# Large experts after small ones: holding back splits until the small expert's last turn, and building one-hot columns a chunk earlier

## Chip, cores, metric

The kernel runs on one core of a Trainium2 chip. The metric is the device time of one execution in microseconds (us).

## What is computed

Two layers of a decoder trunk over 256 tokens of width 1024. Each layer has a mixer (retention, a state-space layer and latent attention side by side) and a feed-forward part. The change lies in the feed-forward part of the second layer, which routes each token to 2 of 8 experts:

```python
def swiglu(h, wg, wu, wd):
    return (jax.nn.silu(h @ wg) * (h @ wu)) @ wd

# routed_ffn, cut
logits = (t @ router)                       # t: 256 x 1024, router: 1024 x 8
top_v, top_i = lax.top_k(logits, 2)
top_w = jax.nn.softmax(top_v, axis=-1)
# the rows of t are gathered by expert; every expert e computes
#   swiglu(rows, wg[e], wu[e], wd[e])       # 1024 -> 3584 -> 1024
# and y[token] += result * weight
```

Each expert has three weight matrices of 1024 x 3584 or 3584 x 1024 in f32, 44 MB for one expert and 352 MB for all eight. All are read once.

## The kernel before

**Slots.** Expert 0 and the seven others, ordered by how many tokens they got, fill eight slots, called experts 0 to 7 here. `KINDS` says which are small (64 columns of tokens: 0, 5, 6, 7) and which large (128 columns: 1 to 4). They are worked off in the order `TURNS`, 0, 1, 2, 5, 3, 6, 4, 7. Three times a large expert follows a small one: 1 after 0, 3 after 5, 4 after 6.

**Chunks.** An expert is done in 7 chunks of 512 of its 3584 inner columns. A chunk reads six pieces of 1 MB: two of `mg` (gate), two of `mu` (up), two of `md` (down). The loop over `turns` in `moe` is a software pipeline written out by hand. One turn does: the gate product of the chunk (`up('mg', ...)`) and Silu of it into `sg` on ACT; the transposes of the previous chunk's hidden rows, `raw_turn` for a small expert (copy `hts` on ACT) or `turn` for a large one (`th` on ACT, `tl` on DVE); the up product (`up('mu', ...)`) and `h = sg * up` on DVE; then the down product of the previous chunk (`raw_down` or `half_down`). After an expert's last chunk `y_parts` (`yh` on ACT, `yl` on DVE) and `scatter` add its result to `acc`. Every engine runs its instructions in the order in which the program issues them.

**Large experts work with split weights.** A small expert multiplies with the f32 pieces as they are. For a large one each half of a piece is first split into two parts, `wh` (cast on ACT) and `wl` (difference on DVE), in `split_half`; each product is then three matmuls (lines 733 to 735). Splits run ahead of their use: `ahead` issues them in the fixed order `porder` as long as fewer than `NH` = 5 halves are alive and the load of the piece has been issued. It is called whenever a half is used up (`w_half`, `w_done`), and with 4 at a small expert's last chunk. In the first chunk of a large expert after a small one, the four halves of `mg` and four of `mu` are split by this, and then, at the end of the gate product, one half of the gate piece of chunk 1. In the ACT queue that cast stands ahead of Silu and of the small expert's last `hts`.

**Loads.** `Stream.pump` issues the loads of pieces on the SP queue in the order of their use. There are 5 staging buffers and 2 more in this stage. One comes free when both halves of its piece are split, or when a small expert's matmuls have read it.

**One-hot columns.** `onehots` builds a 0/1 matrix `gm` on DVE from the slots' positions (one instruction for each of two halves of the tokens). `big_x` and `small_x` gather an expert's tokens with it, as generators of which `advance` runs a step at a time from the list `work`. `side(r)` builds it once more for expert r at chunk 5 (chunk 6 for expert 0) and lets PE transpose it (line 1571) and multiply it with the weights (1572, 1573); the result, `gt` and `ws`, serves `scatter`. The first entry of a turn's `work` runs right after Silu is issued, ahead of the transposes; the others after `h`.

Of the kernel before, what the change touches and what calls it, by code (L numbers as in the profile page):

```python
# [226 lines left out]
class Kernel:  # L227
# [49 lines left out]
    def ahead(self, n=1, E=None):  # L277

        if self.stream.dry:
            return  # L280
        while n and self.pnext < 2 * len(self.porder):
            if self.plive >= self.NH or not self.stream.loaded(self.porder[self.pnext // 2]):
                return
            self.emit_split(E)
            n -= 1

    def emit_split(self, E=None):
        i, j = divmod(self.pnext, 2)
        key = self.porder[i]
        self.parts.setdefault(key, []).append(self.split_half(self.stream.tiles[key][0][0], j, E))  # L290
        self.plive += 1
        self.pnext += 1
        if j:
            self.stream.done(key)
# [18 lines left out]
    def w_done(self, key, ahead=9):  # L313
        if self.stream.dry:
            return
        self.plive -= len(self.parts.pop(key))
        if ahead:
            self.ahead(ahead)

    def w_half(self, key, ahead=9):  # L320

        if self.stream.dry:
            return
        self.parts[key].pop(0)
        self.plive -= 1
        if ahead:
            self.ahead(ahead)
# [1326 lines left out]
    def moe(self, l):  # L1654
        V, S, T = self.V, self.S, self.T
        A, B = self.mod[l, 'Af'], self.mod[l, 'Bf']
        route = self.route(A, B)
        next(route)
        NC = self.NC
        small = lambda r: self.KINDS[r] == 's'  # L1660
        order = self.TURNS
        xg, gts, ys, over = {}, {}, {}, []

        def big_x(r, n):

            X = [self.wkt([128, 8, 256], name, F32R) for name in ("xgh", "xgl")]
            for j in range(n):
                xg[r + j] = [x[:, :, j * 128:(j + 1) * 128] for x in X]
            return self.gather(self.onehots(self.pm[:, :, r:r + n], n, 128), n * 128, A, B, X)

        def small_x(r, n):
            if r:
                x = self.wk.tile([128, 8, n * 64], F32, name="xs")
            else:

                x = self.acc.rearrange("p t d -> p (t d)")[:, :512].rearrange("p (k n) -> p k n", k=8)
            for j in range(n):
                xg[r + j] = x[:, :, j * 64:(j + 1) * 64]
            return self.gather(self.onehots(self.pm[:, :, r:r + n], n, 64), n * 64, A, B, [x])

        def side(r):
            n, w = (2, 64) if small(r) else (1, 128)
            g = self.onehots(self.pm[:, :, r:r + 1].to_broadcast([128, 2, n]), n, w)
            gts[r] = self.slot_side(g, 0, self.wt[:, 0, r:r + 1], self.wt[:, 1, r:r + 1])

        def up(name, r, c, ahead=9):
            p = self.bank("a")
            for i in range(2):
                if small(r):
                    key, w = self.raw_piece(name, c, i, r)  # L1690
                    self.raw_up(p, xg[r], w, i)
                    self.stream.done(key)
                else:
                    key, wh, wl = self.ffn_piece(name, c, i, r)
                    self.half_up(p, xg[r], wh, wl, i, lambda: self.w_half(key))
                    self.w_done(key)
            return p

        self.drain(small_x(0, 1))
        gens = {}  # L1700

        def advance(name, make):
            def f():
                if name not in gens:
                    gens[name] = make()
                next(gens[name], None)
            return f


        work = {(0, 0): [lambda: self.drain(route)],  # L1710
                (0, 1): [lambda: over.extend(self.overflow_list()), self.know_places],
                (0, 2): [advance('s', lambda: small_x(5, 3))] * 3, (0, 3): [advance('s', lambda: small_x(5, 3))] * 3}
        for r in order:
            work.setdefault((r, 5 if r != order[0] else 6), []).append(lambda r=r: side(r))
        for at, b in ((0, 1), (5, 3)):
            for c in (4, 5) if at == 0 else (2, 3):
                work.setdefault((at, c), []).extend([advance(b, lambda b=b: big_x(b, 2))] * 3)

        turns = [(r, c) for r in order for c in range(NC)]
        prev, pend, last = None, [], len(turns) - 1  # L1720
        banks = {}
        free = 'b' + 'dbbb' + 'b' + 'db' + 'b' + 'db' + 'b'
        i = 0
        for r in order:
            n = 1 if small(r) else 2
            banks[r], i = free[i:i + n], i + n

        def scattered(r):
            gt, ws = gts[r]
            if small(r):  # L1730
                yp = self.y_parts(ys[r][0], ws)
                for h in range(2):
                    pend.extend(self.scatter(yp, gt, h, r == 0, slice(64 * h, 64 * h + 64)))

        for n in range(len(turns) + 1):
            cur = turns[n] if n <= last else None
            todo = list(work.get(cur, ()))
            if cur:
                r, c = cur
                w = 256 if small(r) else 512  # L1740
                pg = up('mg', r, c)
                sg = self.wkt([128, 512], "sg")[:, :w]
                S.activation(sg, pg[:, :w], AF.Silu)  # L1743
            if pend:
                pend.pop(0)()
            elif todo:
                todo.pop(0)()
            if prev is not None:
                pr, pc, ph = prev
                ht = (self.raw_turn if small(pr) else self.turn)(ph)  # L1750
            if cur:
                pu = up('mu', r, c)
                h = self.wkt([128, 512], "h")[:, :w]
                V.tensor_mul(h, sg, pu[:, :w])  # L1754
                if small(r) and c == NC - 1 and n < last:
                    self.ahead(4)
            for _ in range(2):
                if pend:
                    pend.pop(0)()
            for f in todo:  # L1760
                f()
            if prev is not None:
                if pc == 0:
                    ys[pr] = [self.bank(t) for t in banks[pr]]
                if small(pr):
                    ps = [self.raw_piece('md', pc, i, pr) for i in range(2)]
                    self.raw_down(ys[pr][0], ht, [w for _, w in ps], pc == 0, pc == NC - 1)
                    for key, _ in ps:
                        self.stream.done(key)
                else:  # L1770
                    for i in range(2):
                        key, wh, wl = self.ffn_piece('md', pc, i, pr)
                        self.half_down(ys[pr][i], ht, wh, wl, pc == 0, pc == NC - 1, lambda: self.w_half(key))
                        self.w_done(key)
                        if pc == NC - 1:
                            gt, ws = gts[pr]
                            pend.extend(self.scatter(self.y_parts(ys[pr][i], ws), gt, i))
                if pc == NC - 1:
                    scattered(pr)
                    for d in (xg, gts, ys):  # L1780
                        d.pop(pr)
            if cur:
                prev = (r, c, h)
        while pend:
            pend.pop(0)()
        self.overflow(A, B, *over)
        o = self.a['out'].rearrange("o (t p) d -> p (o t) d", p=128)
        room = [self.wkt([128, 2, D], name) for name in ("psq", "pyg")]
        for t in range(2):
            hs = [slice(h * 512, (h + 1) * 512) for h in range(2)]  # L1790
            post = self.post(t, [self.acc[:, t, h] for h in hs], self.mod[l, 'Gf'], [r[:, t] for r in room])
            for h, _ in zip(hs, post):
                self.nc.sync.dma_start(o[:, t, h], self.x[:, t, h])
        self.dump(f'xf{l}', self.x.rearrange("p t n -> p (t n)"))
# [89 lines left out]
    def run(self, upto=9):  # L1884
        tc = self.tc
        with ExitStack() as ctx:
# [5 lines left out]
            self.psum = pool(name="psum", bufs=4, space=bass.MemoryType.PSUM)  # L1892
            ctx.enter_context(tc.manual_schedule())
            self.P, self.mod, self.s5, self.b4 = {}, {}, {}, {}
            self.tail = None
            self.c_all, self.c_s5 = ctx, ctx.enter_context(ExitStack())
            self.s5p = self.c_s5.enter_context(tc.tile_pool(name="s5p", bufs=1, side="right"))
# [82 lines left out]
```

## Time and profile before

| | us |
|---|---|
| median of 3 runs | 1485.74 |
| lowest, highest | 1483.95, 1491.18 |
| profiled execution | 1491.5 |
| its span | 1489.7 |

The expert stage begins near 603 us of the span and ends near 1478. The profile shows one execution; times in it count from the start of its span. PE is the matrix engine, ACT casts and does Silu, DVE does elementwise work, SP issues the loads. "PEclk" is the granted clock of PE as a share of 2.4 GHz; 0.50 is 1.2 GHz. In a row of the time order the bracket at the end gives how long the engine was idle before it and what ended that.

### The profile page before, as it was taken

How to read it: one execution, taken by the hardware profiler on the slowest of the kernel's cores; microseconds unless marked ns; L12 is line 12 of the kernel's file. 1: busy time of each engine (PE TensorE's matmuls, PEld its weight loads, DVE VectorE, ACT ScalarE, POOL GpSimd, SP SyncE). 2: the span in 40 equal slices, each digit the busy share in tenths (PEclk: the TensorE clock that was granted, in tenths of full speed). 3: DMA queues.
4: the chain of work that ended last, by engine and by line, in shares of the span. 5: the costliest groups of instructions: out<-in, count | busy, mean ns of one | idle time of the engine just before them, and what ended most of it. 6: DMA issues, size and time to landing. Idle time of an engine off the chain costs nothing. (4 is left out here: it accounts for less than half of the span.)

```text
span 1489.7 us, 21982 instructions
## 1 busy us (share of the span) xinstructions
PE 1390.6 (93%) x8563; PEld 1042.6 (70%) x8563; DVE 848.3 (57%) x1201; ACT 675.4 (45%) x936; POOL 108.9 (7%) x108
## 2 busy tenths in 40 slices
PE   4799789999998999999999999999999998999995
PEld 1676579999997867665687887755687655687652
DVE  4763556656565546313898898522797403897302
ACT  1423444444445244113787877412676202786101
POOL 3201010515021001000000000000000000000000
PEclk9899999999999999799999999999999999999998
DMA  9667794545556484699999998999999999999995
GB/s 305 245 232 277 270 311 183 183 170 172 190 196 242 183 348 184 243 424 424 425 424 403 346 375 334 365 415 425 424 425 378 365 424 425 424 425 354 376 425 207
DMA packets 70078, 482.23 MB, mean 324 GB/s; under 512 B 9800, under 2 KB 10056, under 8 KB 13008
## 3 DMA queue, kind: packets, MB, share of 16 engines
q1 hardware_dynamic: 65952, 473.69, 80.2%
q0 software_dynamic: 3024, 4.75, 1.2%
q10 hardware_dynamic: 992, 2.33, 0.5%
q8 instruction: 69, 1.13, 0.3%
q14 instruction: 41, 0.34, 0.1%
HBM read 479.66 MB, written 1.06 MB: 323 GB/s over the span
## 5 line engine op out<-in xcount | busy, mean ns | idle before, releaser
L274 DVE TENSOR_TENSOR wl<-st,wh 128x1024 fp32r<-128x1024 f32 x464 | 569.6, 1248 | 192.9 <-ACT wh L273 170.0
L273 ACT CAST wh<-st 128x1024 fp32r<-128x1024 f32 x464 | 482.9, 1052 | 274.8 <-PE a L1306 86.4
L733 PE MATMUL a<-wh,xgh 128*128 128x512 f32 x448 | 180.5, 403 | 0.0
L734 PE MATMUL a<-wl,xgh 128*128 128x512 f32 x448 | 177.3, 396 | 2.7 <-DVE wl L274 2.7
L735 PE MATMUL a<-wh,xgl 128*128 128x512 f32 x448 | 176.7, 394 | 0.0
L1593 PE MATMUL a<-st,xs 128*64 128x256 f32 x1344 | 155.1, 381 | 0.9 <-DMA st<-in_mu 0.9
L1593 PEld LDWEIGHTS a<-st,xs 128*64 128x64 f32 x1344 | 95.4, 137 | 57.4 <-issue 12.4
L1305 PE MATMUL a<-hh,wh 128*128 128x256 f32 x448 | 128.2, 286 | 1.9 <-ACT hh L710 1.2
L1743 ACT ACTIVATE sg<-a 128x256 f32<-128x256 f32 (+1 forms) x56 | 27.3, 488 | 224.1 <-PE a L1593 224.1
L1754 DVE TENSOR_TENSOR h<-sg,a 128x256 f32<-128x256 f32 (+1 forms) x56 | 30.8, 551 | 172.1 <-PE a L1593 130.1
L1306 PE MATMUL a<-hl,wh 128*128 128x256 f32 x448 | 127.6, 285 | 0.4 <-DVE hl L711 0.4
L1307 PE MATMUL a<-hh,wl 128*128 128x256 f32 x448 | 127.4, 284 | 0.0
L1610 PE MATMUL b<-st,hts 128*64 128x512 f32 x448 | 110.7, 618 | 13.8 <-ACT hts L1602 9.9
L733 PEld LDWEIGHTS a<-wh,xgh 128*128 128x128 f32 x448 | 85.6, 191 | 22.2 <-issue 2.8
L734 PEld LDWEIGHTS a<-wl,xgh 128*128 128x128 f32 x448 | 85.7, 191 | 21.0 <-DVE wl L274 4.1
L735 PEld LDWEIGHTS a<-wh,xgl 128*128 128x128 f32 x448 | 85.6, 191 | 18.5
L1305 PEld LDWEIGHTS a<-hh,wh 128*128 128x128 f32 x448 | 86.6, 193 | 2.9 <-ACT hh L710 1.4
L1306 PEld LDWEIGHTS a<-hl,wh 128*128 128x128 f32 x448 | 86.6, 193 | 0.8 <-DVE hl L711 0.6
L1307 PEld LDWEIGHTS a<-hh,wl 128*128 128x128 f32 x448 | 86.7, 194 | 0.0
L1610 PEld LDWEIGHTS b<-st,hts 128*64 128x64 f32 x448 | 34.4, 141 | 73.2 <-issue 52.2
L474 PE MATMUL d<-st,c 128*32 128x512 f32 x384 | 53.4, 656 | 23.3 <-DMA st<-in_ada_w 12.1
L337 POOL TENSOR_TENSOR pss<-pss,mhalf 128x1 f32<-128x1 f32 x8 | 5.2, 649 | 890.1 <-DVE pss L336 890.1
(424 smaller groups left out, 1993.7 us busy)
## 6 DMA issues: line engine op xcount, KB each, us to landing
st<-in_mg SPq DMA_DIRECT2D x112, 1024.0 KB, 12.9
st<-in_mu SPq DMA_DIRECT2D x112, 1024.0 KB, 11.6
st<-in_md SPq DMA_DIRECT2D x112, 1024.0 KB, 12.7
st<-in_ada_w SPq DMA_DIRECT2D x48, 1024.0 KB, 7.8
st<-in_fg SPq DMA_DIRECT2D x14, 1024.0 KB, 4.8
st<-in_fu SPq DMA_DIRECT2D x14, 1024.0 KB, 4.8
st<-in_fd SPq DMA_DIRECT2D x14, 1024.0 KB, 4.7
st<-in_w_out SPq DMA_DIRECT2D x8, 1024.0 KB, 7.2
```

The costliest lines, as they stand in the source:

```text
L273: self.S.copy(hi, src)
L274: (E or self.V).tensor_sub(lo, src, hi.bitcast(F32))
L474: self.T.matmul(state['p'][32 * g:32 * g + 32, :], self.c32[:, k, :], st[:, 0, g * 512:(g + 1) * 512], start=(k == 0), stop=(k == 7), skip ...
L733: self.T.matmul(out, xh, wh, start=start, stop=False, skip_group_check=True)
L734: self.T.matmul(out, xh, wl, start=False, stop=False, skip_group_check=True)
L735: self.T.matmul(out, xl, wh, start=False, stop=stop, skip_group_check=True)
L1305: T.matmul(o, wh[:, k, fs], hh[:, kk], start=st, stop=False, skip_group_check=True)
L1306: T.matmul(o, wh[:, k, fs], hl[:, kk], start=False, stop=False, skip_group_check=True)
L1307: T.matmul(o, wl[:, k, fs], hh[:, kk], start=False, stop=(kk == 7), skip_group_check=True)
L1593: self.T.matmul(p[64 * t:64 * t + 64, :256], x[:, 4 * i + k], w[:, k, 256 * t:256 * t + 256], start=(i == 0 and k == 0), stop=(i == 1 and ...
L1610: self.T.matmul(y[64 * i:64 * i + 64, :], ht[:, f % 2, s], ws[i][:, f], start=(first and f == 0), stop=(last and f == 3), skip_group_check ...
L1754: V.tensor_mul(h, sg, pu[:, :w])
```

## The change

Two things are changed in `moe`.

First, when a turn works on a large expert and the previous turn on a small one, `split_up_to` sets a cap, `self.cap`, before the gate product: `ahead` issues no split past the second `mu` piece of that chunk. Once the transposes of the small expert's last chunk and `hts` are issued, the cap is lifted. Splits that a product asks for itself (`w_piece`) don't look at it.

Second, the building of `gm` is parted from its use. `side_hot(r)` does `onehots` in the chunk before the one in which `side(r)` uses it. `big_x` and `small_x` yield between `onehots` and the first step of the gather.

```diff
-        while n and self.pnext < 2 * len(self.porder):
+        while n and self.pnext < min(2 * len(self.porder), self.cap):
...
+    def split_up_to(self, key=None):
+
+        self.cap = 1 << 30 if key is None or self.stream.dry else 2 * self.porder.index(key) + 2
...
-            return self.gather(self.onehots(self.pm[:, :, r:r + n], n, 128), n * 128, A, B, X)
+            g = self.onehots(self.pm[:, :, r:r + n], n, 128)
+            yield
+            yield from self.gather(g, n * 128, A, B, X)
...
-            return self.gather(self.onehots(self.pm[:, :, r:r + n], n, 64), n * 64, A, B, [x])
+            g = self.onehots(self.pm[:, :, r:r + n], n, 64)
+            yield
+            yield from self.gather(g, n * 64, A, B, [x])
+
+        def side_hot(r):
+            n, w = (2, 64) if small(r) else (1, 128)
+            gts[r] = self.onehots(self.pm[:, :, r:r + 1].to_broadcast([128, 2, n]), n, w)
 
         def side(r):
-            n, w = (2, 64) if small(r) else (1, 128)
-            g = self.onehots(self.pm[:, :, r:r + 1].to_broadcast([128, 2, n]), n, w)
-            gts[r] = self.slot_side(g, 0, self.wt[:, 0, r:r + 1], self.wt[:, 1, r:r + 1])
+            gts[r] = self.slot_side(gts[r], 0, self.wt[:, 0, r:r + 1], self.wt[:, 1, r:r + 1])
...
         for r in order:
-            work.setdefault((r, 5 if r != order[0] else 6), []).append(lambda r=r: side(r))
+            c = 5 if r != order[0] else 6
+            work.setdefault((r, c - 1), []).append(lambda r=r: side_hot(r))
+            work.setdefault((r, c), []).append(lambda r=r: side(r))
...
                 w = 256 if small(r) else 512
+                if prev is not None and small(prev[0]) and not small(r):
+                    self.split_up_to(self.ffn_args('mu', c, 1, r)[0])
                 pg = up('mg', r, c)
...
                 ht = (self.raw_turn if small(pr) else self.turn)(ph)
+                self.split_up_to()
```

## Rows read from the trace of the kernel before

**Rows 1.** The page, busy time: engine, busy us and share, instructions.
```profile
PE 1390.6 (93%) x8563; PEld 1042.6 (70%) x8563; DVE 848.3 (57%) x1201; ACT 675.4 (45%) x936; POOL 108.9 (7%) x108
```

**Rows 2.** Stretches of the expert stage: length, engines' busy us, clock, DMA share, GB/s.
```profile
804.00:968.00 164.00, 160.87 (x784) 128.45 (x783) 132.23 (x127) 113.17 (x122) 0.00 (x0) 0.99 0.92 357
...
1136.00:1168.00 32.00, 32.00 (x155) 25.34 (x154) 24.69 (x22) 21.01 (x22) 0.00 (x0) 0.96 0.81 305
1168.00:1354.00 186.00, 177.16 (x982) 120.06 (x981) 95.80 (x98) 81.56 (x98) 0.00 (x0) 0.97 1.01 424
1354.00:1390.00 36.00, 36.00 (x188) 28.02 (x188) 25.53 (x24) 21.87 (x23) 0.00 (x0) 0.96 0.80 304
1390.00:1466.00 76.00, 73.61 (x528) 41.62 (x524) 7.51 (x15) 6.25 (x16) 0.00 (x0) 1.00 1.01 424
```

**Rows 3.** Waits of PE, 600 to 1490 us: us in total, times, longest.
```profile
PE a L1571 <- DVE gm L1522: 10.4, 4, 2.6
PE b L1610 <- ACT hts L1602: 9.9, 4, 3.2
```

**Rows 4.** ACT in order of time, Silu of chunks: start us, duration us.
```profile
790.14 0.59 ACT L1743 ACTIVATE sg<-a 128x512 f32<-128x512 f32 x1
...
810.48 0.59 ACT L1743 ACTIVATE sg<-a 128x512 f32<-128x512 f32 x1
...
913.99 0.59 ACT L1743 ACTIVATE sg<-a 128x512 f32<-128x512 f32 x1
...
935.93 0.59 ACT L1743 ACTIVATE sg<-a 128x512 f32<-128x512 f32 x1
...
1130.55 0.59 ACT L1743 ACTIVATE sg<-a 128x512 f32<-128x512 f32 x1
...
1153.87 0.58 ACT L1743 ACTIVATE sg<-a 128x512 f32<-128x512 f32 x1
...
1332.12 0.59 ACT L1743 ACTIVATE sg<-a 128x512 f32<-128x512 f32 x1
...
1348.90 0.59 ACT L1743 ACTIVATE sg<-a 128x512 f32<-128x512 f32 x1
...
1372.29 0.58 ACT L1743 ACTIVATE sg<-a 128x512 f32<-128x512 f32 x1
```

**Rows 5.** PE in order of time, chunk 5 of expert 1.
```profile
791.75 0.53 PE L1571 MATMUL a<-kc,gm 128*128 128x128 f32 x2 [2.60 <-DVE gm L1522]
...
792.48 0.64 PE L1617 MATMUL a<-kc,h 128*128 128x128 f32 x4
```

**Rows 6.** Stretches around the fourth such wait, columns as in rows 2.
```profile
1332.10:1348.90 16.80, 15.81 (x70) 12.75 (x68) 15.73 (x15) 13.54 (x16) 0.00 (x0) 1.00 1.01 425
...
1352.00:1356.00 4.00, 4.00 (x12) 3.23 (x11) 0.69 (x1) 1.51 (x4) 0.00 (x0) 0.50 0.94 391
```

**Rows 7.** ACT in order of time, from expert 6 to 4.
```profile
1264.13 1.05 ACT L273 CAST wh<-st 128x1024 fp32r<-128x1024 f32 x1 [5.36 <-DMA st<-in_mg]
...
1265.58 0.37 ACT L1602 COPY hts<-a 128x256 f32<-128x256 f32 x1
...
1269.10 1.05 ACT L273 CAST wh<-st 128x1024 fp32r<-128x1024 f32 x1 [0.32 <-DMA st<-in_mu]
```

**Rows 8.** PE in order of time, last down product of experts 0, 5 and 6.
```profile
710.10 3.65 PE L1610 MATMUL b<-st,hts 128*64 128x512 f32 x16 [3.18 <-ACT hts L1602]
...
1048.86 5.35 PE L1610 MATMUL b<-st,hts 128*64 128x512 f32 x16 [3.09 <-ACT hts L1602]
...
1265.99 6.55 PE L1610 MATMUL b<-st,hts 128*64 128x512 f32 x16 [3.11 <-ACT hts L1602]
...
1278.14 0.49 PE L1645 MATMUL a<-yh,gt 64*128 64x512 f32 x1
```

**Rows 9.** DVE in order of time, from expert 6 to 4.
```profile
1266.92 4.63 DVE L274 TENSOR_TENSOR wl<-st,wh 128x1024 fp32r<-128x1024 f32 x4 [0.48 <-ACT wh L273]
1271.47 0.68 DVE L1754 TENSOR_TENSOR h<-sg,a 128x512 f32<-128x512 f32 x1
1273.35 0.75 DVE L1636 SCALAR_TENSOR_TENSOR yl<-b,ws,yh 128x512 fp32r<-128x512 f32 x1 [1.20 <-ACT yh L1635]
```

More of the change, by code (lines that the diff above doesn't have):

```diff
@@ L1894, in run @@
             self.P, self.mod, self.s5, self.b4 = {}, {}, {}, {}
+            self.cap = 1 << 30
             self.tail = None
```

## Prediction, made before the changed kernel was run

> **What bounds the kernel now.** I read the busy shares first: PE is busy 93% of the span [rows 1], which seems to leave little to win. That figure is an average over stages with different limits, so I next read the expert stage in stretches [rows 2]. Look at the last three columns: the granted clock, the share of the DMA engines and the rate. From 1168 to 1354 us and from 1390 to 1466 us the queue of weights runs flat out, at 424 GB/s; the last piece lands near 1468 us and the kernel ends 21 us later. So the end is set by the stream of weights. The stream has a fixed number of bytes, and only the time in which it was not running can be saved. There are three such stretches, all where large experts are at work: 804 to 968 us at 357 GB/s, 1136 to 1168 us at 305, 1354 to 1390 us at 304. Against 424.5 that is (1 - 357/424.5) x 164 = 26.1 us, 9.0 us and 10.2 us of lost transfer. In these stretches PE is busy almost without a break: a staging buffer is free only once its piece has been split, a split needs a buffer that PE gives back, so the stream waits for PE. A stall of PE in a large expert, within such a stretch or before it, delays the stream by its length, up to the transfer that was lost there; elsewhere it costs nothing.
>
> Then I asked which stalls PE has in these experts. The waits of PE name two that belong to the change: 10.4 us in 4 waits for the one-hot columns (gm), and 9.9 us, nearly all of it in three waits, for the ACT copy hts [rows 3].
>
> **Part one: one-hot columns a chunk ahead.** The starts of Silu give the pitch of the chunks [rows 4]. An ordinary chunk of a large expert takes 1348.90 - 1332.12 = 16.78 us. The chunk in which `side` runs takes 810.48 - 790.14 = 20.34 us for expert 1, 21.94 for expert 2, 23.32 for expert 3, 23.39 for expert 4. What `side` adds to PE by itself, from its first transpose to the transposes of `turn`, is 792.48 - 791.75 = 0.73 us, and before it PE sat idle for 2.60 us until DVE had built gm behind its queue of splits [rows 5]. For expert 1 these two explain the longer chunk: 16.78 + 2.60 + 0.73 = 20.1. For experts 2 to 4 there is more: after the stall the granted clock is 0.50, which is 1.2 GHz instead of 2.4, while before it PE ran on at full clock [rows 6]. Built one chunk earlier, the two DVE instructions (0.5 us) lie in the same queue behind the same kind of splits, a whole chunk of 16.78 us before they are read. The stall goes, and with it what sets the clock back. Each such chunk should take 16.78 + 0.73 = 17.5 us, so the gains are 2.8, 4.4, 5.8 and 5.9 us. What the move costs: 0.5 us of DVE in the chunk before, behind which `tl` waits; `tl` is needed only after the 5.6 us of the next mu product, so I cost it at nothing, and at 0.5 us per expert if that cover were gone. For the small experts and for the gathers (`big_x`, `small_x`) the same move lies in stretches where the stream is flat out, so it is worth nothing either way. The gathers used five of their six calls, so the extra yield fits.
>
> **Part two: no fifth split before the small expert's last turn.** At a change from a small to a large expert the ACT queue holds a split of mg for chunk 1 ahead of Silu and ahead of hts. Its weights come late: in expert 4 it starts at 1264.13 us, when the piece has landed, and hts at 1265.58 [rows 7]. PE ended the mu product of chunk 0 at 1265.99 - 3.11 = 1262.88 and stood until hts was there [rows 8]. What would be late next? The `md` pieces of the small expert lie just ahead of that mg piece. Landings are (1269.10 - 1264.13)/2 = 2.5 us apart, so the later `md` piece landed near 1261.6, before PE needs it. Hence `raw_down` could start at 1262.9. It takes 3.65 us at full clock (expert 1), but 5.35 and 6.55 us after the stalls of experts 3 and 4, where the clock fell [rows 8]. So it would end at 1266.5 instead of 1272.5. The next product, mg of chunk 1, runs 1278.14 - 1272.54 = 5.6 us [rows 8]. Its first half would be cast from 1264.13 on, and as Silu and hts no longer stand between the casts, DVE's splits (4 in 4.63 us, [rows 9]) come a little before PE wants them; PE would reach the scatter at 1272.1. There a new, short wait appears: DVE has to split the first half of mu (landed 1269.10, cast 1.05, about 1.2 on DVE: 1271.4), then `h` 0.68 and `yl` 0.75 [rows 9], so the scatter's second matmul may start at about 1272.8, some 0.5 us late. The gains: expert 1, 3.18 - 0.6 = 2.5 us; expert 3, 3.09 + (5.35 - 3.65) - 0.6 = 4.2 us; expert 4, 3.11 + (6.55 - 3.65) - 0.5 = 5.5 us. What the cap takes away is one split run ahead; as the piece lands 5.4 us after ACT ran out of work, that split can't start earlier anyway. The upper end is without the new wait, 0.6 us more each; the lower end, with the wait for mg's splits taking the old one's place, is about 1 us each.
>
> **The sum.** Up to the end of the first lossy stretch (experts 1 and 2): 2.5 + 2.8 + 4.4 = 9.7 us, less than its 26.1, so all of it counts. Expert 3: 4.2 + 5.8 = 10.0 us, but only 9.0 us of transfer were lost: 9.0. Expert 4: 5.5 + 5.9 = 11.4, of which 10.2 count. Together 28.9 us. The profiled execution took 1491.5 us (span 1489.7 and 1.8 around it); 28.9 less is 1462.6. The median of the runs is 1485.7, which gives 1456.8. The two differ by 5.8 us, perhaps because the clock falls in fewer places in some executions; those falls are part of what I subtract, so I subtract from the middle, 1488.6, here and for the rivals: **1460 us**.
>
> The Trainium skill (Perfetto Trace Analysis, Roofline) puts the ceiling of one core's 16 DMA engines at about 435 GB/s. By that figure the two later stretches would have lost 9.6 and 10.8 us instead of 9.0 and 10.2, and the sum would be 30.1. The flat-out rows show 424, which I keep.
>
> **The rivals.**
> *A new wait in place of hts* (1 us gained at each change of expert): 8.2 + 6.8 + 6.9 = 21.9 us, about 1467 us. For it: mg of chunk 1 starts as soon as its first half is split, and the split chain of ACT and DVE begins at the landing, which doesn't move. Against it: at the same pace PE's needs come later than each split.
> *The clock falls anyway*: then only the idle time itself is won, 2.6 us per `side` and 2.5 per change of expert: 7.7 + 5.1 + 5.1 = 17.9 us, about 1471 us. For it: PE still waits for landings at the start of each large expert, a few us before. Against it: through those waits the rows show no fall before the hts stall.
> *One part does not do what it says*: the one-hot part alone gives 18.9, about 1470 us; the cap alone 12.2, about 1476 us.
> *No change*: the lost transfer is not PE's doing but the issuing queue's, and the stream ends when it did. For it: the rate in the lossy stretches is spread over many small dips. Against it: the same queue holds 424 elsewhere.
> *Slower*: with less waiting in large experts, PE meets the small ones with a shorter lead and waits more for landings between their products; the clock falls there. I estimate a small chunk on PE at three products like `raw_down`'s 3.65 us [rows 8], 11 us at full clock, against 14.8 us of the stream (6 landings of 2.5); at half clock some 21, so each chunk caught loses about 6 us. From five such chunks on the gain is gone; eight give 1460 + 48, about 1508 us. Against it: from 1390 to 1466 us, where PE runs small chunks beside a flat-out stream, the clock stays 1.00 [rows 2].
> The Trainium skill (TensorE: Matmul & The Clock Gate, "HAM oscillation") describes such a case, a DMA wait between bursts that sends each next burst to half rate; by that rule this rival would hold, and the last row just named doesn't agree.
>
> **How the numbers follow.** Forecast 0.62, a new wait 0.12, the clock 0.10, one part only 0.06, no change 0.06, slower 0.04. The forecast's own range is 1452 (the median's base, no new waits and no cap by the lost transfer: 1485.7 - 10.3 - 10.6 - 12.0 = 1452.8) to 1466; to hold 8 in 10 I reach to the clock rival: 1452 to 1472. A difference under 0.5% (7.4 us) is about what a measurement of this kernel can't tell from none. Faster by more: 0.62 + 0.12 + 0.10 + 0.06 = 0.90; within it 0.06; slower 0.04.
>
> **What would show it.** In the changed profile: no PE wait for gm in the four large experts and Silu pitches of 17.5 us there; hts on ACT before the first cast of mg's chunk 1, and `raw_down` of about 3.65 us in all three places; clock 1.00 in both; the stream at 424 GB/s nearly throughout from 968 us on, with under 3 us lost. I am wrong if the pitch of those chunks falls but the last landing doesn't move by as much, or if PE stands before mg of chunk 1 instead.

## The result and the profile after

The changed kernel took 1463.54 us (median of 5 executions, 1456.0 to 1465.86) against 1485.74 before: a ratio of 0.9831, 95% interval 0.9804 to 0.9858. In a second comparison, with 19 executions of before, it took 1462.76 against 1491.73: 0.9806, interval 0.977 to 0.9842. (The ratios here and below are those on record; they are not always the quotient of the two medians, which is 0.985 for the first.) It is 22 us faster by the first median, 29 us by the second; the difference lies in the executions of before, which go from 1484 to 1491 us in the first and from 1481 to 1501 us in the second. The profiled execution took 1456.0 us, its span is 1454.2.

The page, busy time, after, against [rows 1]:

```profile
PE 1371.3 (94%) x8563; PEld 1028.3 (71%) x8563; DVE 844.2 (58%) x1201; ACT 672.8 (46%) x936; POOL 108.8 (7%) x108
```

PE does the same matmuls in 19.3 us less. 12.6 us of that lie between the first and the last Silu of the stage, where no step of 4 us shows a clock under 0.99 any more; the other 6.7 us lie ahead of the first Silu. Stretches of the expert stage after, with the columns of [rows 2]:

```profile
804.00:968.00 164.00, 162.41 (x837) 126.51 (x837) 125.68 (x126) 104.88 (x116) 0.00 (x0) 1.00 0.97 384
968.00:1136.00 168.00, 167.88 (x899) 121.26 (x896) 114.98 (x115) 100.40 (x118) 0.00 (x0) 1.00 1.01 424
1136.00:1168.00 32.00, 32.00 (x226) 19.71 (x227) 7.56 (x11) 4.47 (x9) 0.00 (x0) 1.00 1.01 424
1168.00:1354.00 186.00, 181.47 (x988) 128.38 (x985) 114.62 (x113) 98.79 (x113) 0.00 (x0) 1.00 1.01 424
1354.00:1390.00 36.00, 36.00 (x260) 21.29 (x260) 5.00 (x8) 3.65 (x8) 0.00 (x0) 1.00 1.01 425
```

The last column shows where the gain came from. The two later stretches that lost transfer, 305 and 304 GB/s in [rows 2], are gone: from 968 us on the stream of weights runs at 424. Around experts 1 and 2 it rose from 357 to 384 and still loses. Counted in steps of 4 us from 20 us after the first Silu to 8 us after the last, each with (1 - rate/424.5) x 4 and never less than nothing, the stage lost 49.2 us of transfer before and 19.5 after: 29.7 us. The clock column is 1.00 in all five rows.

Waits of PE after, 600 to 1460 us; nothing as long as the two waits of [rows 3] is left:

```profile
PE b L1614 <- DMA st<-in_md: 3.9, 4, 1.3
...
PE a L1545 <- DVE gm L1526: 1.0, 1, 1.0
...
PE b L1614 <- ACT hts L1606: 0.5, 1, 0.5
```

The wait for gm at `side` (10.4 us) is gone altogether; the 1.0 us belongs to a gather. Silu starts of expert 4 after, against the last three of [rows 4]:

```profile
1300.75 0.59 ACT L1757 ACTIVATE sg<-a 128x512 f32<-128x512 f32 x1
...
1317.54 0.59 ACT L1757 ACTIVATE sg<-a 128x512 f32<-128x512 f32 x1
...
1334.94 0.59 ACT L1757 ACTIVATE sg<-a 128x512 f32<-128x512 f32 x1
```

16.79 us for an ordinary chunk, 17.40 for the one with `side`, which was 23.39. From expert 6 to expert 4 after, first ACT, then PE, then DVE, against [rows 7], [rows 8] and [rows 9]:

```profile
1233.45 0.36 ACT L1606 COPY hts<-a 128x256 f32<-128x256 f32 x1
1238.38 1.99 ACT L273 CAST wh<-st 128x1024 fp32r<-128x1024 f32 x2 [4.58 <-DMA st<-in_mg]
```

```profile
1237.06 3.65 PE L1614 MATMUL b<-st,hts 128*64 128x512 f32 x16
...
1246.31 0.50 PE L1649 MATMUL a<-yh,gt 64*128 64x512 f32 x1
1247.02 0.50 PE L1649 MATMUL a<-yl,gt 64*128 64x512 f32 x1 [0.21 <-DVE yl L1640]
```

```profile
1245.62 0.68 DVE L1769 TENSOR_TENSOR h<-sg,a 128x512 f32<-128x512 f32 x1
1246.22 0.74 DVE L1640 SCALAR_TENSOR_TENSOR yl<-b,ws,yh 128x512 fp32r<-128x512 f32 x1
```

hts stands 5 us ahead of the cast that had been before it; `raw_down` starts when the mu product ends and takes 3.65 us instead of 6.55. The short new wait for `yl` is there, 0.21 us here.

### The profile page after: what moved, and what is told of

Read it like the earlier page. It is cut to its first block, busy times and chain, and to the rows that moved or that the text cites. A ratio compares the mean times of both kernels' runs of the same rounds, so it can differ in the third digit from the quotient of the medians.

```text
span 1454.2 us, 21979 instructions
## 1 busy us (share of the span) xinstructions
PE 1371.3 (94%) x8563; PEld 1028.3 (71%) x8563; DVE 844.2 (58%) x1201; ACT 672.8 (46%) x936; POOL 108.8 (7%) x108
## 3 DMA queue, kind: packets, MB, share of 16 engines
HBM read 479.66 MB, written 1.06 MB: 331 GB/s over the span
## 5 line engine op out<-in xcount | busy, mean ns | idle before, releaser
L1614 PE MATMUL b<-st,hts 128*64 128x512 f32 x448 | 106.2, 596 | 6.4 <-DMA st<-in_md 3.9
L739 PEld LDWEIGHTS a<-wh,xgl 128*128 128x128 f32 x448 | 84.1, 188 | 17.9
## 6 DMA issues: line engine op xcount, KB each, us to landing
st<-in_mu SPq DMA_DIRECT2D x112, 1024.0 KB, 14.8
```

What stands on the lines that cost most here:

```text
L739: self.T.matmul(out, xl, wh, start=False, stop=stop, skip_group_check=True)
L1614: self.T.matmul(y[64 * i:64 * i + 64, :], ht[:, f % 2, s], ws[i][:, f], start=(first and f == 0), stop=(last and f == 3), skip_group_check ...
```

## The experiments

All were compared with the kernel before; the first four ran together, and so did the last four, without the changed kernel; what they are said to be over it is counted from its 1462.76 us. "Lost transfer" is counted in steps of 4 us as above. "Stage" is the time from the first Silu (expert 0, chunk 0) to expert 7's first Silu, read from the trace.

**The changed kernel again.**

> The changed kernel as it is, to have more executions and a second trace. My account: in the expert stage, from the first Silu to the Silu of expert 7's first chunk, 31 to 33 us less than in the trace of before (770.7 us there), in this execution as in the first; the chunks with side at 17.4 us; what differs between executions of this kernel (1456 to 1466 us) lies ahead of the first Silu, which came at 611.0 us in the first trace and 615.6 in that of before. Rival: the executions differ inside the expert stage, because the clock falls in some of them at other places; then the stage is 5 to 9 us longer here and a chunk or two shows a granted clock of 0.5. The median over before should stay at 1463 against 1486, 22 to 23 us less.

Median 1462.76 us. First Silu of expert 0 and of expert 7, from the trace of before:

```profile
615.61 0.38 ACT L1743 ACTIVATE sg<-a 128x256 f32<-128x256 f32 x1 [4.47 <-PE a L1593]
...
1386.31 0.39 ACT L1743 ACTIVATE sg<-a 128x256 f32<-128x256 f32 x1 [3.92 <-PE a L1593]
```

from the first trace of the changed kernel:

```profile
611.01 0.38 ACT L1757 ACTIVATE sg<-a 128x256 f32<-128x256 f32 x1 [4.55 <-PE a L1597]
...
1348.97 0.38 ACT L1757 ACTIVATE sg<-a 128x256 f32<-128x256 f32 x1 [3.92 <-PE a L1597]
```

and from the second:

```profile
614.08 0.38 ACT L1757 ACTIVATE sg<-a 128x256 f32<-128x256 f32 x1 [4.72 <-PE a L1597]
...
1353.59 0.38 ACT L1757 ACTIVATE sg<-a 128x256 f32<-128x256 f32 x1 [3.92 <-PE a L1597]
```

The stage takes 738.0 and 739.5 us, against 770.7 before: 31 to 33 us less, as expected. The spans differ by 6.0 us: 3.1 ahead of the first Silu, 1.5 in the stage, the rest behind it. So about half of the difference between these two lies ahead of the stage that was changed. The clock falls nowhere in the stage. One wait is longer than in the first trace, that for `yl` at the change to expert 4:

```profile
1251.63 0.50 PE L1649 MATMUL a<-yl,gt 64*128 64x512 f32 x1 [1.06 <-DVE yl L1640]
```

In the ten traces of this study the first Silu comes between 611.0 and 620.6 us.

**Only the one-hot columns.**

```diff
-                if prev is not None and small(prev[0]) and not small(r):
-                    self.split_up_to(self.ffn_args('mu', c, 1, r)[0])
```

> The changed kernel without the cap: only the one-hot columns are built a chunk ahead. My account: the four chunks with side fall to 17.4 us, 2.9 + 4.5 + 5.9 + 6.0 = 19.4 us less than before by their pitches, and all of it reaches the end, as each stretch that lost transfer lost more than that: 17 to 20 us faster than before. The three waits for hts stay at 3.1 us each, with the clock falling after those at experts 3 and 4. Rival (the stream takes it back, or the falls come anyway): under 12 us.

1475.62 us, 16.1 less than before (ratio 0.988, interval 0.9834 to 0.9926). The four chunks with `side` have 17.4 us; 31.1 us of transfer are lost, 18.1 less than before. The three waits for hts, PE in order of time:

```profile
712.34 6.55 PE L1614 MATMUL b<-st,hts 128*64 128x512 f32 x16 [3.18 <-ACT hts L1606]
...
1046.49 5.03 PE L1614 MATMUL b<-st,hts 128*64 128x512 f32 x16 [3.09 <-ACT hts L1606]
...
1257.28 5.35 PE L1614 MATMUL b<-st,hts 128*64 128x512 f32 x16 [3.12 <-ACT hts L1606]
```

They stay, and this time the clock fell after all three, after the first as well (0.50 from 712 to 716 us), which it had not done in the trace of before. The median gain of 16.1 us is a little under the expected 17 to 20; the recorded ratio makes it 17.9, and in the trace the stage is 18.3 us shorter than before. The rival (under 12 us) is out by the trace; the interval alone, 11 to 25 us, nearly rules it out. The earlier columns of the gathers were not run by themselves; PE's waits for those columns are 2.0 us in the trace of before, 1.0 and 2.0 in the two of the changed kernel.

**Only the cap.**

```diff
-            g = self.onehots(self.pm[:, :, r:r + n], n, 128)
-            yield
-            yield from self.gather(g, n * 128, A, B, X)
+            return self.gather(self.onehots(self.pm[:, :, r:r + n], n, 128), n * 128, A, B, X)
...
         def side(r):
+            side_hot(r)
...
-            work.setdefault((r, c - 1), []).append(lambda r=r: side_hot(r))
```

> The changed kernel with side, big_x and small_x as before: only the cap. My account: the waits for hts go, 2.5 + 4.2 + 5.5 = 12.2 us, all of it reaching the end: 10 to 13 us faster than before; the four waits for gm stay at 2.6 us. With the one-hot part alone it adds up to more than both together gain, since the lost transfer of the later stretches caps the sum. Rival (another wait in place of hts, 1 us won at each): 3 us faster, which is the same within the measurement.

1478.80 us, 12.9 less (ratio 0.9906, interval 0.9871 to 0.9942); 34.2 us of transfer lost, 15.0 less than before. The wait for gm is as it was, but what follows it isn't always the same. Chunk 5 of expert 1 and of expert 2, Silu starts:

```profile
789.90 0.59 ACT L1753 ACTIVATE sg<-a 128x512 f32<-128x512 f32 x1
813.08 0.59 ACT L1753 ACTIVATE sg<-a 128x512 f32<-128x512 f32 x1
...
916.59 0.59 ACT L1753 ACTIVATE sg<-a 128x512 f32<-128x512 f32 x1
936.90 0.58 ACT L1753 ACTIVATE sg<-a 128x512 f32<-128x512 f32 x1
```

In expert 1 the chunk takes 23.2 us, in expert 2 20.3; experts 3 and 4 had 23.3 and 20.3. In the trace of before it was 20.3, 21.9, 23.3 and 23.4. The PE row and the stretch after the wait in expert 1, and then the stretch after the same wait in the trace of before:

```profile
791.51 0.69 PE L1575 MATMUL a<-kc,gm 128*128 128x128 f32 x2 [2.60 <-DVE gm L1526]
```

```profile
792.00:796.00 4.00, 4.00 (x15) 3.52 (x15) 0.69 (x1) 1.02 (x3) 0.00 (x0) 0.50 1.01 426
```

```profile
792.00:796.00 4.00, 4.00 (x24) 3.45 (x24) 1.07 (x2) 2.15 (x5) 0.00 (x0) 1.00 1.01 426
```

The same wait of 2.60 us ([rows 5] has that of before) is followed by a granted clock of 0.50 in one execution and by full clock in another.

**PE busy during the wait.**

```diff
+            if not small(r):
+                p = self.bank("a")
+                for i in range(10):
+                    T.matmul(p, self.xnh[:, 0, :128], self.xnh[:, 0, :512], start=True, stop=True)
             gts[r] = self.slot_side(g, 0, ...)
```

> The kernel before, and in the chunk with side of each large expert ten matmuls of 512 columns whose result nobody reads, issued ahead of the transposes, so that PE works through the wait for gm instead of standing (10 x 0.227 = 2.3 us). It separates the clock from the wait. My account: the wait is no shorter than what the matmuls take, but the clock stays at 1.00 after it, so the chunks with side come to 16.8 + 2.6 + 0.7 = 20.1 us in all four large experts: 0.2 + 1.8 + 3.2 + 3.3 = 8.5 us faster than before, 5 to 9 us. Rival (the clock falls because of the small matmuls and transposes of side, not because of the wait): chunks of 22 to 23.4 us as before and no gain.

1484.36 us, 7.4 less (ratio 0.9958, interval 0.9931 to 0.9984). All four chunks with `side` take 20.3 us. PE in chunk 5 of expert 4, and the stretch after it:

```profile
1338.86 2.43 PE L1687 MATMUL a<-xnh 128*128 128x512 f32 x10
1341.73 0.44 PE L1571 MATMUL a<-kc,gm 128*128 128x128 f32 x2 [0.44 <-DVE gm L1522]
```

```profile
1344.00:1348.00 4.00, 4.00 (x19) 3.34 (x18) 2.71 (x3) 2.98 (x3) 0.00 (x0) 1.00 1.01 412
```

The transposes come as late as before, but the clock stays at 1.00. Nor do the transposes alone set it back: in the traces of the changed kernel they run in the same four chunks without a wait, and these take 17.4 us. So it is PE's standing still that sets the clock back, though not each time (it fell after five of the eight such waits in the traces of before and of the cap alone), and the clock is a cost of its own: up to 3 us on top of a wait of 2.6.

**More PE work in the small experts.** The edit stands in the turn, between the transposes and the up product; the next two use the same lines with another condition and 24 matmuls (`r == 1 and c == 3`, `r in (3, 4) and c == 3`).

```diff
+            if cur and r in (5, 6, 7):
+                p = self.bank("a")
+                for _ in range(12):
+                    T.matmul(p, self.xnh[:, 0, :128], self.xnh[:, 0, :512], start=True, stop=True)
             if cur:
                 pu = up('mu', r, c)
```

> The changed kernel, and in each chunk of the small experts 5, 6 and 7 twelve more matmuls of 512 columns whose result nobody reads (12 x 0.227 = 2.7 us, 57 us of PE in all). A small chunk takes PE 10.9 us and the stream 14.8, so with 13.6 us PE still waits for the stream. My account (from 940 us on the stream sets the end): 3 to 10 us over the changed kernel, for the first chunks of each expert, where PE is behind, and the last one. Rival (PE, 94% busy, sets the end): about 57 us more.

1504.80 us: 42 us over the changed kernel, and slower than before (ratio 1.0106, interval 1.0065 to 1.0147). The expectation missed by far. Three stretches of this run:

```profile
968.00:1136.00 168.00, 166.98 (x927) 118.34 (x924) 96.30 (x101) 83.60 (x101) 0.00 (x0) 1.00 0.99 408
...
1168.00:1354.00 186.00, 186.00 (x1050) 129.15 (x1050) 93.50 (x96) 79.65 (x94) 0.00 (x0) 1.00 0.99 412
...
1390.00:1466.00 76.00, 76.00 (x516) 46.62 (x514) 7.09 (x14) 5.48 (x14) 0.00 (x0) 1.00 0.97 395
```

PE is busy through the whole of the last two, and the stream no longer reaches 424. The count in steps gives 64.9 us of lost transfer, but some 12 us of that lie behind the last piece, which landed early in this step:

```profile
1472.00:1476.00 4.00, 4.00 (x24) 2.97 (x24) 0.00 (x0) 0.76 (x2) 0.00 (x0) 1.00 0.05 20
```

So about 53 us of transfer are lost, and the kernel ends 31 us after that landing where the changed kernel takes 21: in expert 7 PE itself is what is waited for. The comparison of one small chunk (10.9 us of PE, 14.8 of the stream) was the wrong one: a small expert works off the lead that the large one before it, with 16.8 to 17.6 us a chunk, let the stream build. What counts is the pair. From the first Silu of expert 5 to that of expert 6 this run took 108.8 + 117.0 = 225.8 us without a wait of PE; less the 7 x 2.7 = 18.9 added, PE's own work is 206.9 us, as much as the pair takes in the changed kernel (90.5 + 116.4) and as 84 landings of 2.47 us make (1 MB at 424.5 GB/s), 207. PE has no room there. Experts 6 and 4 leave it 103.1 + 117.0 - 18.9 = 201.2 of 208.4. Neither the account nor the rival held: of the 57 us added, PE could take some 15 without delay.

**More PE work in expert 1.**

> The changed kernel, and in chunk 3 of the large expert 1 24 more matmuls (5.4 us) whose result nobody reads. My account: 15 to 16 us of transfer are still lost around experts 1 and 2, because PE is late there, so the delay counts in full: 5.4 us over the changed kernel, lost transfer 21 us in the trace. Rival (the stream hides it as elsewhere): under 2 us.

1469.59 us, 6.8 over the changed kernel. The chunk takes 22.2 us instead of 16.8, and 24.3 us of transfer are lost in all, 22.0 of them up to expert 5's fourth chunk where the changed kernel loses 16.9. The stretch around experts 1 and 2, in the changed kernel and in this run:

```profile
800.00:980.00 180.00, 178.41 (x944) 136.85 (x943) 131.73 (x134) 110.37 (x124) 0.00 (x0) 1.00 0.97 387
```

```profile
800.00:980.00 180.00, 178.41 (x914) 138.14 (x914) 137.65 (x137) 115.35 (x128) 0.00 (x0) 1.00 0.96 375
```

The delay of 5.4 us counts in full, within the scatter of a few us.

**More PE work in experts 3 and 4.**

> The changed kernel, and in chunk 3 of the large experts 3 and 4 24 more matmuls (5.4 us each) whose result nobody reads. In these the stream now runs flat out, with PE ahead of what it needs by the part of the gain that the cap of the sum cut off. My account: 5.4 less 1 to 2 us each, so 7 to 9 us over the changed kernel, and as much lost transfer in the trace where there is none now. Rival (PE sets the pace there): 10.9 us. Rival (the stream has room to spare): under 3 us.

1468.62 us, 5.9 over. Around expert 3 and from expert 4 on 5.0 and 4.6 us of transfer are lost, where it was 0.7 and 1.8: 7.1 us of the 10.9. Stretches at the two experts, in the changed kernel and in this run:

```profile
1100.00:1200.00 100.00, 100.00 (x634) 67.00 (x632) 42.51 (x46) 35.17 (x45) 0.00 (x0) 1.00 1.01 424
1310.00:1420.00 110.00, 108.82 (x698) 71.32 (x698) 41.36 (x45) 34.72 (x47) 0.00 (x0) 1.00 1.01 423
```

```profile
1100.00:1200.00 100.00, 100.00 (x605) 69.84 (x605) 51.72 (x55) 43.14 (x53) 0.00 (x0) 1.00 0.99 407
1310.00:1420.00 110.00, 110.00 (x673) 75.70 (x673) 53.77 (x58) 44.49 (x55) 0.00 (x0) 1.00 0.99 410
```

By the trace this is the lower edge of what was expected; by the median it is a little less. The scatter of a few us leaves the first rival (10.9) unlikely, not out. The second, room to spare, is out by the trace.

**One staging buffer fewer.**

```diff
-                self.pools(c1, dict(h8=5, f4=0, f2=6, f1=3), 2)
+                self.pools(c1, dict(h8=5, f4=0, f2=6, f1=3), 1)
```

> The changed kernel with 6 staging buffers in the expert stage instead of 7. If the remaining loss around experts 1 and 2 is a lead that the buffers can't hold, one piece (2.5 us of the stream) less of lead costs 2.5 us more there, and up to 2.5 us at each of experts 3 and 4, where the lead is now just held: 4 to 7 us over the changed kernel. Rival (the loss there comes from the queue that issues the loads): no change.

1471.57 us, 8.8 over; the trace loses 26.4 us, 6.9 more: 3.2 up to expert 5's fourth chunk, 2.5 around expert 3 and 1.3 from expert 4 on. The median is above what was expected; the lost transfer agrees with the account. The stretch around experts 1 and 2 in this run, where the changed kernel has 387 GB/s:

```profile
800.00:980.00 180.00, 178.41 (x908) 140.05 (x907) 141.02 (x140) 118.00 (x129) 0.00 (x0) 1.00 0.96 379
```

The rival (no change) is out: the loss around experts 1 and 2 grows with a buffer less, as a lead that the buffers can't hold would. That it would shrink with a buffer more is not shown.

## Why the prediction was right

**The stream sets the end.** It did: lost transfer fell by 29.7 us in the trace, and the sum had 28.9. The stretches at experts 3 and 4, which by the sum had 9.0 and 10.2 us to give, gave 9.4 and 9.7 by the count in steps; the first gave 10.7 where the sum had 9.7. From 968 us on under 3 us are lost. That the stream is what sets the end holds only together with PE, as is said below. Neither of the two signs of being wrong shows: counted from the first Silu the last bytes land about 31 us earlier than before, and PE doesn't stand before `mg` of chunk 1 at any of the three changes.

**The chunks with `side`.** 17.40 us in all four, forecast 17.5. Gains 2.9, 4.5, 5.9 and 6.0 us against the trace of before. No cost of the earlier columns shows.

**The changes of expert.** From the time at which `raw_down` could start to the start of the next mu product, before and after: expert 1 13.54 and 10.83 us, expert 3 15.10 and 10.70, expert 4 16.33 and 10.80. The gains are 2.7, 4.4 and 5.5 where the working had 2.5, 4.2 and 5.5. The new wait for `yl` is 0.2 to 0.3 us there, not 0.5; in the second trace it is 1.06 us at expert 4, which takes about 0.9 us of that gain back.

**The cap on the sum.** By the chunks and the changes just listed, expert 3 gained 4.4 + 5.9 us and expert 4 5.5 + 6.0, together 21.8; the stream got back 9.4 + 9.7 = 19.1 there. So 2.7 us were cut off, by the forecast's own working 2.2. Each part alone saved 18.1 and 15.0 us of transfer, together 33.1, and both together 29.7. That comparison is of single traces, in which the clock did not fall at the same places: with the cap alone the four chunks with `side` were 1.9 us shorter in sum than before, with the columns alone the three last down products 1.4 us longer. In the medians (16.1 + 12.9 against 29.0) the cap is too small to see.

**The base.** The prediction took 1488.6 us, between the profiled execution and the median, and landed at 1460 for a measured 1463.5. The gain of the first comparison, 22 us, is smaller than the 28.9 of the sum; that of the second, 29.0, is equal to it, which is partly luck, since the two compare the same kernels. The guess that the clock falls in fewer places in some executions can't be seen place by place, as there is one trace of before. What is on record agrees with it: over the 26 executions of before in the last two comparisons the mean granted clock goes with the time, from 0.976 at 1481.0 us to 0.964 at 1501.4. And in the traces the same wait cost 20.3 us a chunk or 23.3. So what a part with such a wait gains has a scatter of a few us for each wait, and one profile of before is a sample of it.

**What was wrong.** The working of the slower rival compared a small chunk on PE with six landings and saw PE at 11 of 14.8 us. The run with more work in the small experts shows that over a large and a small expert PE and the stream are level. The number didn't rest on it, but the sentence that outside the lossy stretches a stall of PE "costs nothing" is half of the truth: in the changed kernel both count, and PE has nothing to spare at experts 5 and 3. Of the other rivals, a new wait in place of hts shows only as the 1.06 us named above; one part without effect and no change show nowhere. The clock fell nowhere in the stage, the small experts included, in the two traces of the changed kernel, but in the run with more work in expert 1, which leaves the end of expert 6 as it is, it fell once, after waits for landings there:

```profile
1230.53 5.34 PE L1614 MATMUL b<-st,hts 128*64 128x512 f32 x14 [1.30 <-DMA st<-in_md]
```

In the second trace of the changed kernel the same waits were followed by full clock:

```profile
1224.94 3.65 PE L1614 MATMUL b<-st,hts 128*64 128x512 f32 x14 [1.30 <-DMA st<-in_md]
```

The flat-out rows after show 424 and 425 GB/s, so the measured rate was the one to count with. The Trainium skill (Perfetto Trace Analysis, Roofline) bounds a core that works alone by its 16 DMA engines, at about 435 GB/s. The trace stays a little under that.

## What to carry to other kernels

On ACT a cast that waited for a load held up the short copy behind it, and PE with it, for 3.1 to 3.2 us at each change of expert. So look in an engine's queue for small copies on which another engine waits, and let work that runs ahead stop in front of them. Where a stream of loads sets the end, count the transfer lost around a stall to see what the stall is worth: it bounds the sum of all the stalls removed there, and two parts can save less together than the sum of what each saves alone. When stages alternate between one that gains a lead and one that uses it up, compare the engines over the pair, not over one chunk.

## What the runs showed of the hardware

The same wait of PE, 2.60 us at the same place in the program, was followed by full clock or by half clock (0.50, 1.2 GHz), with chunks of 20.3 or 23.2 to 23.4 us (once 21.9), in different experts of one execution and in the same expert of executions of two kernels. With PE kept busy through all but 0.4 us of it, the clock stayed at 1.00 in all four. A shorter wait can be followed by a fall too: 14 matmuls behind a wait of 1.3 us, itself shortly after two of 0.4 and 0.6 us, took 5.34 us in one trace and 3.65 in another. A stream of 1 MB loads ran at 424 to 425 GB/s for hundreds of us, at a busy share of 1.01 of the DMA engines.
